# Two stages of a seven-product down projection change places in a one-core decoder trunk

## The chip, the cores and the metric

The kernel runs on one NeuronCore of a Trainium2 chip. The metric is the device time of one execution in microseconds (us), the median of the runs shown. A core has engines that work side by side, each on its own list of instructions in its own order: TensorE (PE in the profile) for matmuls, VectorE (DVE), ScalarE (ACT), GpSimd (POOL), and SyncE (SP), which here issues nearly all DMA transfers. Engines wait for each other by semaphores.

## The reference, cut to what matters

The program is a trunk of two layers on 1024 tokens of width 1024. Layer 0 mixes tokens by retention and RWKV-7 heads, layer 1 by sliding-window attention. Each mixer is followed by a dense SwiGLU network, and the end is an RMS norm:

```
def swiglu(h, w_gate, w_up, w_down):
    return (jax.nn.silu(h @ w_gate) * (h @ w_up)) @ w_down
...
        n = rms_norm(h, norm2_g[layer])
        h = h + swiglu(n, ffn_w_gate[layer], ffn_w_up[layer], ffn_w_down[layer])
    return rms_norm(h, final_g)
```

The inner width D_FF is 2816, that is 22 tiles of 128. The change is in the last product, the one with `w_down`, of both layers.

## The kernel before

Activations are kept transposed: 128 features on the partitions, 512 tokens (one half of the sequence) along the free axis. So `h` has eight tiles for each half, `h0` and `h1`, and the hidden activation has 22 for each half, stored in DRAM (`hid`).

**Split operands.** Every fp32 operand of a matmul is split into a high part, which the matmul can take exactly, and the low rest. A product is three matmuls: high by high, high by low, low by high (`prod`, lines 1188 to 1193). The high part of a weight is a cast on ScalarE (line 1378), the low part a subtract on GpSimd (line 1379), both in `vsplit`. The high part of an activation is a cast on ScalarE (line 356), its low part a subtract on GpSimd or on VectorE by turns (line 358), in `split`.

**Seven products for eight.** The down projection takes the weights and the activations as two by two blocks: rows even or odd (output tiles 2i and 2i+1), columns even or odd (hidden tiles 2p and 2p+1), and the two halves of the tokens. A Winograd form needs seven block products instead of eight, with sums of weights and sums of activations. The blocks of a weight are a11, a12, a21, a22; the sums are s1 = a21 + a22, s2 = s1 - a11, s3 = a11 - a21 and s4 = a12 - s2, formed on VectorE (line 1405). The activation sums (`hc`) were formed and split earlier and are read back from DRAM, already split, by `sums8` (line 1384). Plain activations are read raw from `hid` into the tiles `hr` by `plain8` (line 1389) and split then. Activations X stand in a ring of twelve places (`place`; tiles `n` and `ha` in the profile), `hr` has four.

**Groups and stages.** `down` (lines 1408 to 1488) goes through three groups of columns (4, 4 and 3 pairs, `DGROUPS`). Each group has seven stages, and each stage four blocks of output (`dps`), with 4 pairs 12 matmuls of 128x128 by 128x512 for a block and 48 for a stage. The stages before the change:

1. a11 with the plain even tiles of half 0, into PSUM banks A; a copy `u0` of A on ScalarE (line 1442); VectorE forms s1 and s2 of each block.
2. s2 with activation sum 2, into banks B; B + u0 goes to `h1`; VectorE forms s3 = a11 - a21.
3. a12 with the plain odd tiles of half 0, added to banks A; A goes to `h0`; VectorE forms s4 = a12 - s2 in the place of s2.
4. s3 with activation sum 3, added to B.
5. a22 with activation sum 4, added to B.
6. s1 with activation sum 1, into new banks A.
7. s4 with the plain odd tiles of half 1, added to A.

**What sets the order.** The text of `down` gives an order; a scheduler then places the instructions of each engine by a time model of its own, so engines may take work of the next stages ahead of work of this one. DMA issues marked `keep` stay in program order on SP. `behind` puts an instruction behind another: the copies `u0` stand behind the last weight cast of stage 1 (line 1442). Split weights stand in a ring of six tiles (`w` and `wr`). Each DMA holds one of eight semaphores, so that at most eight are under way on SP.

In the first group of a layer the activations of stage 1 and the weights of its first two blocks are prepared ahead, during the last step of the gate and up products (`first_x`). The weights of the down projection (tiles `wd`) are loaded when their memory gets free, near the start of the first group. At that time VectorE still has the last sums of the gate and up products to form (lines 1200, 1250, 1326). Layer 0's first group begins near 1129 us after the start of the span, layer 1's near 2100 us.

Of the kernel before, what the change touches and what calls it, by code (L numbers as in the profile page):

```python
# [13 lines left out]
ALU = mybir.AluOpType  # L14
# [190 lines left out]
class Kern:  # L205
# [462 lines left out]
    def pair(self, u, hf, p):  # L668
# [124 lines left out]
        for w in range(2):  # L793
# [4 lines left out]
            mean = self.t(mp, [P, 32], "vm", 2)[:, :8].rearrange("p (a b) -> p a b", b=2)  # L798
            V.tensor_reduce(out=mean, in_=ps, axis=AX.X, op=ALU.add, negate=True)

# [33 lines left out]
    def unit(self, u, hf, pairs):  # L834
# [10 lines left out]
        for q in range(2):  # L845
            nc.sync.dma_start(DT[64 * q : 64 * q + 64], dn)
        X = self.t(mp, [P, 16, 32], "X", 1)
        Xf = X.rearrange("p a b -> p (a b)")
        G.memset(Xf, 0.0)
# [4 lines left out]
        for j in range(31):  # L854
            n, m = j // 2 + 1, 31 - j
            tv = tmp[:, : n * m].rearrange("p (a b) -> p a b", b=m)
            V.tensor_tensor(
                out=tv, in0=X[:, 0:n, j : j + 1].to_broadcast([P, n, m]),
                in1=DT[:, j : j + 1, j + 1 : 32].to_broadcast([P, n, m]), op=ALU.mult,
            )  # L860
            V.tensor_tensor(out=X[:, 0:n, j + 1 : 32], in0=X[:, 0:n, j + 1 : 32], in1=tv, op=ALU.add)
            if j % 2:
                yield (), 1.9
        for q in range(2):
            nc.sync.dma_start(dg.rearrange("u (i q) t -> q u i t", q=2)[q], X[64 * q : 64 * q + 64])
        if u:
# [541 lines left out]
    def down(self, L, fp, fz, rest, X, first):  # L1408


        op, S = self.vop, self.nc.scalar
        h0, h1 = (self.kt(self.h[hf]) for hf in range(2))
        dps = range(KT // 2)
        j, ends = len(X), []

        def place():
            nonlocal j
            i, j = j % 12, j + 1
            if i >= 8:
                return self.t(fp, [P, 2, HT], "ha", 4, F32R)  # L1420
            return self.t(self.nb, [P, 2, HT], "n8", 8, F32R)

        def plain(hf, f):
            return self.plain8(L, hf, f, place(), self.t(fp, [P, HT], "hr", 4))

        for gi, g in enumerate(DGROUPS):
            n, ps = g[1] - g[0], range(*g)
            ta, tb = ("fffy", "mmrc")[:: 1 - 2 * (gi % 2)]
            s1, u0, a1 = [], [], []
            W = [self.wdown(L, 0, g, fp, "wd0", 5)]  # L1430
            X = X or [plain(0, 2 * p) for p in ps]
            W += [self.wdown(L, 2 * i, g, fp, "wd0", 5) for i in (1, 2, 3)]
            for i in dps:
                W[i] += self.wdown(L, 2 * i + 1, g, fp, "wd1", 5)
            A = [self.pst(t, [P, HT]) for t in ta]
            first += [self.vsplit(W[dp][0]) for dp in dps[len(first) :]]
            cast = self.last_cast
            for dp in dps:
                a11, a12, a21, a22 = W[dp]
                self.prod(A[dp], first[dp], X, True, False)  # L1440
                u0.append(self.t(fz, [P, HT], "u0", 4))
                self.behind(S.copy(u0[dp], A[dp]), cast)
                s1.append(op(self.wsum(fp, n, 4, 8), a21, a22))
                if ends:
                    self.behind(self.last_vop, ends[dp])
                a1.append(a11)
                W[dp][0] = op(self.wsum(fp, n, 4, 8), s1[dp], a11, ALU.subtract)
            X = [self.sums8(L, p, 2, place()) for p in ps]
            B = [self.pst(t, [P, HT]) for t in tb]
            for dp in dps:  # L1450
                self.prod(B[dp], self.vsplit(W[dp][0]), X, True, False)
                y = op(self.t(fz, [P, HT], "y", 2), B[dp], u0[dp])
                op(h1(2 * dp), h1(2 * dp), y)
                op(W[dp][2], a1[dp], W[dp][2], ALU.subtract)
            X = [plain(0, 2 * p + 1) for p in ps]
            for dp in dps:
                self.prod(A[dp], self.vsplit(W[dp][1]), X, False, True)
                op(h0(2 * dp), h0(2 * dp), A[dp])
                op(W[dp][0], W[dp][1], W[dp][0], ALU.subtract)
            X = [self.sums8(L, p, 3, place()) for p in ps]  # L1460
            for dp in dps:
                self.prod(B[dp], self.vsplit(W[dp][2]), X, False, False)
                y = op(self.t(fz, [P, HT], "y", 2), B[dp], u0[dp])
                op(h1(2 * dp + 1), h1(2 * dp + 1), y)
            X = [self.sums8(L, p, 4, place()) for p in ps]
            while self.owed:
                self.keep(self.nc.sync.dma_start(*self.owed.pop(0)))
            for _ in rest:
                pass
            for dp in dps:  # L1470
                self.prod(B[dp], self.vsplit(W[dp][3]), X, False, True)
                op(u0[dp], B[dp], u0[dp])
                op(h0(2 * dp + 1), h0(2 * dp + 1), u0[dp])
            X = [self.sums8(L, p, 1, place()) for p in ps]
            X6 = [plain(1, 2 * p + 1) for p in ps]
            if g[1] == NP:
                yield
            A = [self.pst(t, [P, HT]) for t in ta]
            for dp in dps:
                self.prod(A[dp], self.vsplit(s1[dp]), X, True, False)  # L1480
                op(h1(2 * dp + 1), h1(2 * dp + 1), A[dp])
            ends, first = [], []
            for dp in dps:
                self.prod(A[dp], self.vsplit(W[dp][0]), X6, False, True)
                op(h1(2 * dp), h1(2 * dp), A[dp])
                ends.append(self.last_vop)
            X = ()
        yield
# [399 lines left out]
```

## Time and profile before

| | |
|---|---|
| median of 3 runs | 2331.51 us (2331.47 to 2333.43) |
| the profiled execution, by its own time | 2330.62 us |
| its span, first to last instruction | 2328.6 us |
| mean granted TensorE clock | 0.996 of full speed |
| DMA, mean over the span | 175 GB/s |

The span lies inside the execution's time, with 2.0 us around it. Times within the trace are counted from the start of the span. In a timeline a row gives start, duration, engine, line, operation, output and inputs, the count, and in brackets the idle time ahead of it with what ended it. Several instructions of a kind in a row stand as one row with a count. A busy TensorE is what the profile models from the starts of the matmuls; where matmuls follow each other without a pause, their starts are a fixed step apart, though each lasts longer than the step.

### The profile page before, as it was taken

The page shows a single profiled execution, that of the slowest core. Times are in us where ns is not written, and L with a number is a line of the kernel's source. Part 1 is how long each engine was busy: PE and PEld are TensorE (multiplying, and loading weights), DVE is VectorE, ACT ScalarE, POOL GpSimd, SP SyncE. Part 2 cuts the span into 40 slices and gives each one's busy share as a digit, 9 for nine tenths or more (in the row PEclk, how much of TensorE's full clock was granted, in tenths as well). Part 3 has the DMA queues.
Part 4 walks back from the last instruction along what each step waited for, and adds up shares of the span by engine and source line. Part 5 has one row for each costly group of instructions (what it writes and reads, how often), then busy time and mean ns, then how long its engine had stood idle before and what let it go on. Part 6 is the DMA issues. An engine that isn't in the chain of part 4 may idle for free.

```text
span 2328.6 us, 35662 instructions
## 1 busy us (share of the span) xinstructions
PE 2289.3 (98%) x13056; PEld 1816.4 (78%) x13056; DVE 1704.2 (73%) x2667; ACT 1044.2 (45%) x1943; POOL 979.8 (42%) x764
## 2 busy tenths in 40 slices
PE   8999999999999999999999999999999999999998
PEld 6777777777778888888788887777788888887886
DVE  6876865875667358888885957877647788888766
ACT  5454434424455333333343456666645333343335
POOL 3132221211341067777776500002102677776775
PEclk9999999999999999999999999999999999999999
DMA  7665553433445555555666331113236466656663
GB/s 276 207 210 194 189 152 127 138 119 112 148 173 191 201 167 207 209 208 214 249 257 216 107 127 64 57 64 122 96 128 224 159 222 218 214 200 252 249 217 113
DMA packets 170622, 407.46 MB, mean 175 GB/s; under 512 B 43216, under 2 KB 45904, under 8 KB 170448
## 3 DMA queue, kind: packets, MB, share of 16 engines
q1 hardware_dynamic: 167040, 398.63, 49.9%
q10 hardware_dynamic: 2832, 4.45, 0.5%
q8 instruction: 104, 1.70, 0.3%
q0 software_dynamic: 576, 2.10, 0.2%
q14 instruction: 70, 0.57, 0.1%
HBM read 276.53 MB, written 123.21 MB: 172 GB/s over the span
## 4 chain that ended last, share of the span: by engine, by line
PE 69%; DVE 5%; ACT 2%; issue 1%; POOL 0%; DMA 0%; DVEq 0%; POOLq 0%; ACTq 0%
PE ps_m L1191 7%; PE ps_m L1192 7%; PE ps_m L1193 7%; PE ps_f L350 4%; PE ps_f L351 4%; PE ps_f L352 4%; PE ps_f L1191 4%; PE ps_f L1193 4%; PE ps_f L1192 4%; PE ps_r L1191 2%; PE ps_r L1193 2%; PE ps_r L1192 2%; PE ps_c L1193 2%; PE ps_c L1192 2%; PE ps_c L1191 2%; PE ps_m L240 2%
## 5 line engine op out<-in xcount | busy, mean ns | idle before, releaser
L240 PE MATMUL ps_f<-n,w 128*128 128x512 f32 x1440 | 379.3, 411 | 8.9 <-ACT w L335 5.7
L240 PEld LDWEIGHTS ps_f<-n,w 128*128 128x128 f32 x1440 | 266.6, 190 | 91.4 <-issue 21.8
L336 POOL TENSOR_TENSOR w<-wr,w 128x512 fp32r<-128x512 f32 x63 | 85.9, 1368 | 523.9 <-ACT w L335 520.1
L335 ACT CAST w<-wr 128x512 fp32r<-128x512 f32 x231 | 142.1, 619 | 178.0 <-PE ps_f L352 76.7
L336 DVE TENSOR_TENSOR w<-wr,w 128x512 fp32r<-128x512 f32 x168 | 120.7, 722 | 68.2 <-ACT w L335 67.9
L336 POOL TENSOR_TENSOR w<-wq,w 128x512 fp32r<-128x512 f32 x91 | 130.3, 1442 | 31.9 <-ACT w L335 31.9
L1191 PE MATMUL ps_m<-n,w 128*128 128x512 f32 x333 | 130.9, 393 | 0.0
L1193 PE MATMUL ps_m<-n,w 128*128 128x512 f32 x333 | 130.2, 391 | 0.4 <-POOL w L1379 0.4
L1192 PE MATMUL ps_m<-n,w 128*128 128x512 f32 x333 | 130.1, 391 | 0.0
L350 PE MATMUL ps_f<-n,w 128*128 128x512 f32 x320 | 127.3, 399 | 0.0
L1200 DVE TENSOR_TENSOR nq<-ps_m,u 128x512 f32<-128x512 f32 x88 | 58.9, 684 | 93.3 <-PE ps_m L1193 93.3
L351 PE MATMUL ps_f<-n,w 128*128 128x512 f32 x320 | 126.9, 396 | 0.0
L352 PE MATMUL ps_f<-n,w 128*128 128x512 f32 x320 | 126.6, 396 | 0.0
L1191 PE MATMUL ps_f<-n,w 128*128 128x512 f32 x287 | 113.7, 396 | 0.0
L1193 PE MATMUL ps_f<-n,w 128*128 128x512 f32 x287 | 112.1, 392 | 0.0
L1192 PE MATMUL ps_f<-n,w 128*128 128x512 f32 x287 | 111.7, 389 | 0.0
L358 POOL TENSOR_TENSOR n<-nq,n 128x512 fp32r<-128x512 f32 x60 | 100.0, 1677 | 7.6 <-ACT n L356 7.6
L1379 POOL TENSOR_TENSOR w<-wd,w 128x512 fp32r<-128x512 f32 (+1 forms) x62 | 85.1, 1379 | 38.9 <-ACT w L1378 37.2
L1191 PE MATMUL ps_m<-cb,w 128*128 128x512 f32 x236 | 91.9, 389 | 0.3 <-DVE nq L1200 0.3
L1379 POOL TENSOR_TENSOR w<-ws,w 128x512 fp32r<-128x512 f32 (+1 forms) x48 | 71.8, 1502 | 47.8 <-ACT w L1378 47.8
L1192 PE MATMUL ps_m<-cb,w 128*128 128x512 f32 x236 | 91.8, 389 | 0.0
L1193 PE MATMUL ps_m<-cb,w 128*128 128x512 f32 x236 | 91.8, 389 | 0.0
(520 smaller groups left out, 6456.9 us busy)
## 6 DMA issues: line engine op xcount, KB each, us to landing
hc<-n SPq DMA_DIRECT2D x84, 512.0 KB, 2.8
wsp<-w SPq DMA_DIRECT2D x54, 512.0 KB, 3.4
w<-wsp SPq DMA_DIRECT2D x54, 512.0 KB, 3.5
n<-hc SPq DMA_DIRECT2D x54, 512.0 KB, 5.6
wq<-in_w_gate SPq DMA_DIRECT2D x44, 512.0 KB, 4.4
u<-u SPq DMA_DIRECT2D x88, 256.0 KB, 3.1
wr<-in_w_in SPq DMA_DIRECT2D x34, 512.0 KB, 4.9
ha<-hc SPq DMA_DIRECT2D x34, 512.0 KB, 5.7
```

The costliest lines, as they stand in the source:

```text
L240: self.nc.tensor.matmul(out, lhsT, rhs, **kw)
L335: nc.scalar.copy(hi[:, :n], raw[:, c])
L336: self.lo.tensor_tensor(out=lo[:, :n], in0=raw[:, c], in1=hi.bitcast(F32)[:, :n], op=ALU.subtract)
L350: nc.tensor.matmul(ps, hi, rh, start=k == 0, stop=False)
L351: nc.tensor.matmul(ps, hi, rl, start=False, stop=False)
L352: nc.tensor.matmul(ps, lo, rh, start=False, stop=k == n - 1)
L358: e.tensor_tensor(out=lo, in0=src, in1=hi.bitcast(F32), op=ALU.subtract)
L1191: mm(ps, hi, xh, start=first and k == 0, stop=False, skip_group_check=True)
L1192: mm(ps, hi, xl, start=False, stop=False, skip_group_check=True)
L1193: mm(ps, lo, xh, start=False, stop=last and k == len(w) - 1, skip_group_check=True)
L1200: self.last_add = V.tensor_tensor(out=o, in0=x, in1=y, op=ALU.add)
L1379: nc.gpsimd.tensor_tensor(out=lo, in0=v, in1=hi.bitcast(F32), op=ALU.subtract)
```

## The change

Stages 2 and 3 exchange their places in all three groups of both layers: the product of a12 with the plain odd tiles of half 0 now follows stage 1, and the product of s2 with activation sum 2 comes third. The sum s3 is now formed in the text with the second stage, s4 with the third.

```diff
                 W[dp][0] = op(self.wsum(fp, n, 4, 8), s1[dp], a11, ALU.subtract)
+            X = [plain(0, 2 * p + 1) for p in ps]
+            for dp in dps:
+                self.prod(A[dp], self.vsplit(W[dp][1]), X, False, True)
+                op(h0(2 * dp), h0(2 * dp), A[dp])
+                op(W[dp][2], a1[dp], W[dp][2], ALU.subtract)
             X = [self.sums8(L, p, 2, place()) for p in ps]
             B = [self.pst(t, [P, HT]) for t in tb]
             for dp in dps:
                 self.prod(B[dp], self.vsplit(W[dp][0]), X, True, False)
                 y = op(self.t(fz, [P, HT], "y", 2), B[dp], u0[dp])
                 op(h1(2 * dp), h1(2 * dp), y)
-                op(W[dp][2], a1[dp], W[dp][2], ALU.subtract)
-            X = [plain(0, 2 * p + 1) for p in ps]
-            for dp in dps:
-                self.prod(A[dp], self.vsplit(W[dp][1]), X, False, True)
-                op(h0(2 * dp), h0(2 * dp), A[dp])
                 op(W[dp][0], W[dp][1], W[dp][0], ALU.subtract)
             X = [self.sums8(L, p, 3, place()) for p in ps]
```

## The prediction

> **What bounds the kernel now.** I read the profile's page first, then windows around the two down projections, then the timelines of the engines there.
>
> ```profile
> span 2328.6 us, 35662 instructions
> PE 2289.3 (98%) x13056; PEld 1816.4 (78%) x13056; DVE 1704.2 (73%) x2667; ACT 1044.2 (45%) x1943; POOL 979.8 (42%) x764
> 1139.70:1144.40 4.70, 2.08 (x8) 0.94 (x6) 4.70 (x6) 1.20 (x2) 2.22 (x3) 1.00 1.04 411
> 1146.00:1340.00 194.00, 194.00 (x857) 160.65 (x856) 153.91 (x179) 77.71 (x137) 133.85 (x93) 1.00 0.56 199
> 2111.00:2115.30 4.30, 1.98 (x9) 1.09 (x7) 4.30 (x6) 1.36 (x3) 1.82 (x3) 1.00 1.04 412
> 2115.30:2118.70 3.40, 3.40 (x9) 2.62 (x10) 3.40 (x3) 0.37 (x1) 3.21 (x2) 0.51 1.03 422
> 2119.00:2300.00 181.00, 181.00 (x800) 149.87 (x799) 141.56 (x158) 75.18 (x130) 127.95 (x90) 1.00 0.57 204
> ```
>
> After the window and its length a row gives PE, PEld, DVE, ACT and POOL busy, then clock, DMA share and GB/s. TensorE is the bound. In the down projections it is fully busy (194.00 of 194.00, 181.00 of 181.00) except right behind the first stage of the first group of each layer. One matmul takes 194.00/857 = 0.226 us. The change touches six groups, but only these two places, with PE busy 2.08 of 4.70 and 1.98 of 4.30, have idle time to win.
>
> ```profile
> 1139.49 0.39 PE L1193 MATMUL ps_y<-n,w 128*128 128x512 f32 x1
> 1139.71 0.39 PE L1191 MATMUL ps_m<-n,w 128*128 128x512 f32 x1
> ...
> 1141.91 0.50 PE L1193 MATMUL ps_m<-n,wr 128*128 128x512 f32 x1 [0.72 <-POOL wr L1379]
> 1144.32 0.50 PE L1191 MATMUL ps_r<-n,wr 128*128 128x512 f32 x1 [1.90 <-ACT wr L1378]
> ```
>
> ```profile
> 2111.09 0.39 PE L1191 MATMUL ps_m<-n,w 128*128 128x512 f32 x1
> ...
> 2112.80 0.50 PE L1193 MATMUL ps_m<-n,w 128*128 128x512 f32 x1 [0.41 <-POOL w L1379]
> 2115.20 0.69 PE L1191 MATMUL ps_r<-n,w 128*128 128x512 f32 x1 [1.90 <-ACT w L1378]
> ```
>
> From the first matmul of stage 2 to the seventh are six steps. Layer 0 took 1144.32 - 1139.71 = 4.61 for 6 x 0.226 = 1.36: **3.25 lost**. Layer 1 took 4.11: **2.75 lost**, and then 3.40 us at clock 0.51, another 3.40 x 0.49 = **1.67**. Together 7.7 us, 0.33%: no gain can be larger.
>
> What ends last there is VectorE, which forms s1, s2 and s3 of each block:
>
> ```profile
> 1133.90:1138.30 4.40, 4.40 (x21) 3.66 (x20) 4.26 (x7) 1.69 (x3) 0.00 (x0) 1.00 1.02 419
> 1131.01 1.67 DVE L1326 TENSOR_TENSOR n<-n,n 128x512 f32<-128x512 f32 x1
> ...
> 1138.33 0.69 DVE L1405 TENSOR_TENSOR ws<-ws,wd 128x512 f32<-128x512 f32 x1
> 1138.94 1.78 DVE L1405 TENSOR_TENSOR wd<-wd,wd 128x512 f32<-128x512 f32 x1
> 1140.65 1.76 DVE L1405 TENSOR_TENSOR ws<-wd 128x512 f32<-128x512 f32 x1
> ...
> 1143.64 0.62 ACT L1378 CAST wr<-ws 128x512 fp32r<-128x512 f32 x1 [3.14 <-DVE ws L1405]
> ```
>
> ```profile
> 1130.38 3.44 POOL L1379 TENSOR_TENSOR w<-wd,w 128x512 fp32r<-128x512 f32 x2
> 1138.38 1.80 POOL L1379 TENSOR_TENSOR w<-ws,w 128x512 fp32r<-128x512 f32 x1 [4.56 <-ACT w L1378]
> 1140.14 1.72 POOL L1379 TENSOR_TENSOR wr<-ws,wr 128x512 fp32r<-128x512 f32 x1
> ```
>
> See two things. While POOL does nothing (0.00 from 1133.90 to 1138.30) VectorE does an operation in 4.26/7 = 0.61 us; beside a POOL subtract the same kind takes 1.78 and 1.76. And a subtract beside VectorE takes 1.72 (3.44/2). So where both work without pause, each finishes about one operation in 1.72. POOL's pause of 4.56 us is what lets VectorE reach s2 of the second block by 1139.02.
>
> **The change part by part.** No operation is added or removed: 48 matmuls, 4 weight casts and subtracts, 4 loads change places, and 4 activation splits come a stage earlier. The scheduler decides what that does, so I read the order of the built program. During stage 1 of layer 0 POOL now has six subtracts in a row (four of a12, two of stage 1), then s2 of blocks 0 and 1, then activations X0 and X2 (X1 and X3 are VectorE's). In layer 1 the two of stage 1 come first and the rest in one row. ScalarE has, behind stage 1: copy of u0 of block 3, cast of s2 of block 1, and only then the casts of X0 to X3. That is the new wait: stage 2's own activations stand, on ScalarE and again on POOL, behind a weight sum of the stage that was moved back, and TensorE waits for them.
>
> Stage 2 now adds into the PSUM banks that the copies of u0 read. The last copy runs from 1139.91 (row below), 0.6 long, ahead of X0's cast in any case: no cost.
>
> Loads: the four hr are issued ahead of the four sums, right behind the last weight.
>
> ```profile
> 1139.91 0.59 ACT L1442 COPY u<-ps_y 128x512 f32<-128x512 f32 x1 [0.23 <-PE ps_y L1193]
> 1148.72 1.66 ACT L356 CAST ha<-hr 128x512 fp32r<-128x512 f32 x3
> 1131.36 0.45 SPq L1384 DMA_DIRECT2D n<-hc  x1
> wd<-in_w_down SPq DMA_DIRECT2D x1, 512.0 KB, 5.8
> n<-hc SPq DMA_DIRECT2D x1, 512.0 KB, 6.6
> ```
>
> The last two rows are the last weight's load, issued at 1130.89, and the first sum's, at 1131.36; they land at 1136.7 and 1138.0: 1.3 us per 512 KB, 0.65 for an hr of 256 KB. So X0 lands near 1137.4 and X3 near 1139.3, the first sum 1.3 later; all before their casts. SP's queue keeps its order apart from this exchange. I cost the loads at nothing; the cover is ScalarE's queue, and if that were free X0 could still be cast at 1137.4.
>
> *Layer 0.* POOL: 1130.38 + 6 x 1.72 = 1140.70, no pause. The fourth of them ends at 1137.26; stage 1's last block needs it for its third matmul, nine ahead of the one at 1139.49, at 1137.45. Stage 1 just holds. VectorE has nine operations from 1131.01 to s2 of block 1. At 1.72, 5.6 of them are done by 1140.70; the other three and a bit take 3 x 0.61 and one subtract of POOL in between (1.27, row in (b)): 1143.8 instead of 1139.02. The cast of s2 then starts at 1143.8, that of X0 0.52 later (three casts take 1.66, one 0.62), and 0.62 after that the first matmul can go: 1145.0, **5.3 after stage 1**. Four matmuls (high half of X0 for four blocks) last until 1145.9. X0's low half stands on POOL behind s2 of block 1: 1144.45 + 2 x 1.72 = 1147.9, **2.0 more**. Then 18 matmuls, 4.1, to 1152.0. X1's low half is the ninth VectorE operation after 1143.8: 3.4 of them until POOL pauses at 1144.45 + 3 x 1.72 = 1149.6, the rest at 0.61, 1153.0: **1.0 more**. Sum 8.3 against 3.25: +5.05.
>
> *Layer 1.*
>
> ```profile
> 2105.84 0.59 ACT L1442 COPY u<-ps_f 128x512 f32<-128x512 f32 x1 [2.13 <-PE ps_f L1193]
> 2111.28 0.59 ACT L1442 COPY u<-ps_y 128x512 f32<-128x512 f32 x1 [0.72 <-PE ps_y L1193]
> 2107.28 0.69 DVE L1405 TENSOR_TENSOR ws<-ws,wd 128x512 f32<-128x512 f32 x1
> ```
>
> The four casts of a12 stand behind the copy of 2105.84, so POOL starts at 2107.0 and then has eight subtracts without pause: s2 of block 0 done at 2107.0 + 5 x 1.72 = 2115.6, of block 1 at 2117.3, X0 at 2119.0, X2 at 2120.8. VectorE ends s2 of block 0 at 2107.9 and three operations later, at 1.72, s2 of block 1: 2113.1. X0's cast ends at 2114.25: **3.2** after stage 1's end at 2111.09. Four matmuls, then six of the third stage, the last waiting for 2117.3: **1.0**; then X0's low half: **1.45**; three matmuls; then X1's, the eighth on VectorE: 4.5 at 1.72 until 2120.8, 3.5 at 0.61, 2122.9: **3.15**. Sum 8.8 against 2.75: +6.05.
>
> *Clock.* Layer 1 keeps its 1.67. In layer 0 the trace shows none, with 0.72 and 1.90 idle; with 5.3 it may come. Bounds 0 and +1.67; part of the slow matmuls would stand ahead of another wait, so I take +0.8. The low bound of the term in layer 1 is -1.67, if the gaps fall so that the clock stays.
>
> The page "TensorE: Matmul & The Clock Gate" of the Trainium skill (section "What's actually happening") says the clock halves after an idle window of about 3.4 us and recovers after a busy one. By that rule layer 0 would pay a whole term; layer 1 here fell after idle times of 0.41 and 1.90 alone, and layer 0 did not after 0.72 and 1.90, so the trace does not bear out 3.4 us as the threshold.
>
> *Elsewhere.* In groups two and three plain activations now come in three stages in a row (last, first, second). Six POOL subtracts at 1.72 are 10.3 of a stage of 48 x 0.226 = 10.9: hidden, with 0.5 spare per stage. Cost 0; if the cover fails, some 1 us at each of four places.
>
> **Sum:** 5.05 + 6.05 + 0.8 = +11.9 on the profiled execution's 2330.62 (span 2328.6 and 2.0 around it): 2342.5. The runs' median, 2331.51, is 0.9 higher, so I say **2343**.
>
> **Rivals.**
>
> (a) *The change does what it says*: a block without sums covers VectorE, and VectorE does not suffer from POOL's longer run. It decides if VectorE keeps 0.61 beside POOL. Then only the fixed order holds. Layer 0: copy at 1139.91, two casts, 0.5 + 0.5 + 0.62, first matmul 1141.6 (1.85), X0's low half at 1141.05 + 2 x 1.27 = 1143.6 (1.15): 3.0 against 3.25. Layer 1: 2111.28 + 1.64 = 2112.9 (1.85), X0's low half at 2107.0 + 7 x 1.27 = 2115.9 (0.6): 2.45 against 2.75. With the clock unchanged -0.55, with it kept up -2.2: 2329.3 to 2331. For it: loads are in time, a12 needs no sum. Against: 1.78 and 1.76 above. This ends not slower, and it can't reach 0.2% faster.
>
> (b) *VectorE is shut out altogether while POOL runs on*, not one for one.
>
> ```profile
> 1109.90 7.71 DVE L358 TENSOR_TENSOR n<-wq,n 128x512 fp32r<-128x512 f32 x1
> 1109.53 2.54 POOL L358 TENSOR_TENSOR n<-wq,n 128x512 fp32r<-128x512 f32 x2
> ```
>
> This one lasted through a run of POOL operations without pause, which took only 1.27 each (2.54/2). Layer 0 hardly changes (POOL's six end at 1138.0, eight operations follow at 0.61, again about 1143 to 1144). In layer 1 VectorE would wait until 2107.0 + 5 x 1.27 = 2113.4, s2 of block 1 come at 2115.2, X0 at 2116.3, X1 near 2124.4: some 3 more, 2346. Against: in the quoted stage itself the two alternate.
>
> (c) *Clock falls at both places and again after the second gaps*: +1.7 to +3.3 on top, 2344 to 2346.
>
> (d) *The later groups lose their cover* (three plain stages in a row): +4, 2347.
>
> **How the numbers follow.** Forecast 0.66, (a) 0.08, (b) 0.08, (c) 0.12, (d) 0.06. A measurement of this kernel tells about 0.2% (4.7 us) from no change, so "same" ends at 2336.2. A half effect (VectorE at 1.2 instead of 1.72 beside POOL) gives about +6, 2337.5, and is in the forecast's share; with the clock's term at its low bound, 2335. That is the lower end; the upper is (b) and (c) together, 2349. Outside is (a), 0.08, and a little at each end. Of (a) I give 0.01 to faster, should its 2329.3 still come out lower, and 0.07 to same; with 0.02 from the weakest of the forecast: faster 0.01, same 0.09, slower 0.90.
>
> **What would show it.** Right: ahead of the first matmul of line 1191 with ps_f and hr's activations, idle time of 3 to 6 us released by ScalarE (n, line 356); a second wait released by POOL (line 358) and one by VectorE (line 358); sum operations of line 1405 at 1.7 from 1131 to 1140; POOL without pause there. Wrong: X0 cast before the copy at the end of stage 1, VectorE operations at 0.6 to 0.7 beside POOL, PE idle under 3.5 us at both places, or new idle time in groups two and three.

## The result, and the profile after

The changed kernel takes **2343.62 us** (median of 6 runs, 2342.48 to 2346.38); the kernel before 2332.79 (6 runs, 2331.47 to 2338.15). The ratio is 1.0048, 95% interval 1.0038 to 1.0059: about 11 us slower (0.0038 to 0.0059 of 2332.79 is 8.9 to 13.8). 2343 was forecast.

First the page of the changed kernel: its span, and the busy times of the engines.

```profile
span 2344.2 us, 35684 instructions
PE 2295.2 (98%) x13056; PEld 1820.7 (78%) x13056; DVE 1696.3 (72%) x2667; ACT 1043.7 (45%) x1943; POOL 984.8 (42%) x764
```

The same 13056 matmuls, the same 2667, 1943 and 764 operations: no work of these kinds was added (the 22 instructions more in all are none of them), so the time is idle time or slow matmuls. One caution on reading the span. The profiled execution itself took 2346.03, 15.4 more than that of before, and 3.9 of this was lost before the down projection was reached, in code that both kernels share. The first activation of layer 0's gate shows it, first in the kernel before, then in the kernel after (timeline of ScalarE; start, duration):

```profile
716.31 0.60 ACT L1246 ACTIVATE sg<-ps_f 128x512 f32<-128x512 f32 x1
```

```profile
720.24 0.60 ACT L1246 ACTIVATE sg<-ps_f 128x512 f32<-128x512 f32 x1
```

So times below are compared within a stage, never from the start of the span.

The windows of the kernel after: length, then PE, PEld, DVE, ACT and POOL busy, clock, DMA share, GB/s.

```profile
1143.60:1149.20 5.60, 0.29 (x2) 0.00 (x0) 5.57 (x6) 2.20 (x5) 2.93 (x3) 1.00 1.03 421
1149.29:1152.70 3.41, 2.69 (x6) 1.68 (x7) 3.41 (x3) 1.51 (x3) 3.41 (x3) 0.50 1.02 419
1152.70:1156.10 3.40, 3.40 (x10) 2.64 (x9) 3.40 (x5) 0.00 (x0) 1.02 (x1) 0.51 0.24 99
1160.00:1350.00 190.00, 190.00 (x840) 157.34 (x839) 142.22 (x173) 74.24 (x130) 127.52 (x88) 1.00 0.55 195
2120.40:2124.80 4.40, 0.15 (x1) 0.00 (x0) 4.37 (x3) 1.70 (x4) 4.40 (x4) 1.00 1.02 417
2124.88:2128.90 4.02, 4.02 (x11) 3.15 (x12) 3.99 (x4) 1.51 (x3) 4.02 (x3) 0.58 0.86 351
...
2132.50:2135.90 3.40, 3.37 (x8) 2.67 (x9) 1.78 (x3) 0.00 (x0) 0.00 (x0) 0.53 0.00 0
2136.00:2310.00 174.00, 174.00 (x769) 144.07 (x768) 123.49 (x147) 67.07 (x116) 120.73 (x83) 1.00 0.59 212
```

TensorE does nothing for 5.60 us in layer 0 and 4.40 in layer 1, where VectorE is busy throughout (5.57 of 5.60, 4.37 of 4.40). Behind that come stretches with a clock of 0.50 to 0.58, two of them in each layer. From 1160 and from 2136 TensorE is fully busy again, through groups two and three: the later groups cost nothing. The timeline of TensorE in the kernel after names what ended its waits:

```profile
1149.29 0.80 PE L1191 MATMUL ps_f<-n,w 128*128 128x512 f32 x1 [5.41 <-ACT n L356]
...
1152.09 0.79 PE L1192 MATMUL ps_f<-n,w 128*128 128x512 f32 x1 [0.72 <-POOL n L358]
...
2120.16 0.39 PE L1193 MATMUL ps_y<-n,w 128*128 128x512 f32 x1
2124.88 1.20 PE L1191 MATMUL ps_f<-n,w 128*128 128x512 f32 x3 [4.33 <-ACT n L356]
...
2132.53 0.79 PE L1192 MATMUL ps_f<-n,w 128*128 128x512 f32 x1 [2.81 <-DVE n L358]
```

Before, the waits at these places were 0.72 and 1.90, and 0.41 and 1.90. The chain behind the first wait of layer 0, from the timelines of ScalarE, then VectorE, then GpSimd in the kernel after:

```profile
1145.76 0.58 ACT L1442 COPY u<-ps_y 128x512 f32<-128x512 f32 x1
1148.10 0.62 ACT L1378 CAST w<-ws 128x512 fp32r<-128x512 f32 x1 [1.77 <-DVE ws L1405]
1148.63 2.17 ACT L356 CAST n<-hr 128x512 fp32r<-128x512 f32 x4
```

```profile
1141.68 1.78 DVE L1405 TENSOR_TENSOR ws<-wd 128x512 f32<-128x512 f32 x1
1143.49 1.65 DVE L1405 TENSOR_TENSOR ws<-ws,wd 128x512 f32<-128x512 f32 x1
1145.07 0.68 DVE L1405 TENSOR_TENSOR wd<-wd,wd 128x512 f32<-128x512 f32 x1
...
1146.38 1.63 DVE L1405 TENSOR_TENSOR ws<-ws,wd 128x512 f32<-128x512 f32 x1
```

```profile
1139.46 5.13 POOL L1379 TENSOR_TENSOR w<-wd,w 128x512 fp32r<-128x512 f32 x3
1145.93 1.54 POOL L1379 TENSOR_TENSOR w<-ws,w 128x512 fp32r<-128x512 f32 x1 [1.33 <-ACT w L1378]
```

Read from the bottom. GpSimd runs without pause until 1144.6 (1139.46 + 5.13). VectorE's operations take 1.65 to 1.78 until then, 0.68 in GpSimd's pause behind it, and 1.63 again beside GpSimd's next subtract (1145.93). The last row of VectorE, s2 of the second block, is done at 1148.01; its cast starts at 1148.10, having waited 1.77 for it; the casts of the activations X, four of them, start at 1148.63 behind that cast; and the matmul at 1149.29 waited for the first of them. A matmul that needs no sum stands still for a sum, because the sum's cast is ahead of its own in ScalarE's queue.

### The profile page after: what moved, and what is told of

It is laid out like the page before. It is cut to its first block, busy times and chain, and to the rows that moved or that the text cites. A ratio compares the mean times of both kernels' runs of the same rounds, so it can differ in the third digit from the quotient of the medians.

```text
span 2344.2 us, 35684 instructions
## 1 busy us (share of the span) xinstructions
PE 2295.2 (98%) x13056; PEld 1820.7 (78%) x13056; DVE 1696.3 (72%) x2667; ACT 1043.7 (45%) x1943; POOL 984.8 (42%) x764
## 4 chain that ended last, share of the span: by engine, by line
PE 79%; DVE 11%; ACT 4%; DMA 3%; issue 2%; SPq 1%; POOL 0%; DVEq 0%; ACTq 0%; POOLq 0%
PE ps_m L1191 8%; PE ps_m L1193 8%; PE ps_m L1192 8%; PE ps_f L240 7%; PE ps_m L240 5%; PE ps_f L350 4%; PE ps_f L351 4%; PE ps_f L352 4%; PE ps_f L1192 4%; PE ps_f L1193 4%; PE ps_f L1191 4%; PE ps_r L1193 2%; PE ps_c L1193 2%; PE ps_r L1192 2%; PE ps_c L1192 2%; PE ps_r L1191 2%
## 5 line engine op out<-in xcount | busy, mean ns | idle before, releaser
L240 PE MATMUL ps_f<-n,w 128*128 128x512 f32 x1440 | 379.4, 412 | 8.8 <-ACT w L335 5.9
L1191 PE MATMUL ps_f<-n,w 128*128 128x512 f32 x309 | 123.4, 401 | 9.7 <-ACT n L356 9.7
L350 PE MATMUL ps_f<-n,w 128*128 128x512 f32 x320 | 127.0, 399 | 0.0
L351 PE MATMUL ps_f<-n,w 128*128 128x512 f32 x320 | 127.0, 397 | 0.0
L352 PE MATMUL ps_f<-n,w 128*128 128x512 f32 x320 | 126.6, 396 | 0.0
L1192 PE MATMUL ps_f<-n,w 128*128 128x512 f32 x309 | 121.4, 393 | 3.5 <-DVE n L358 2.8
L1191 PE MATMUL ps_m<-n,w 128*128 128x512 f32 x318 | 124.6, 392 | 0.0
L1192 PE MATMUL ps_m<-n,w 128*128 128x512 f32 x318 | 123.8, 389 | 0.0
L1193 PE MATMUL ps_m<-n,w 128*128 128x512 f32 x318 | 123.7, 389 | 0.0
L1193 PE MATMUL ps_f<-n,w 128*128 128x512 f32 x309 | 121.2, 394 | 0.0
L1379 POOL TENSOR_TENSOR w<-wd,w 128x512 fp32r<-128x512 f32 (+1 forms) x62 | 90.8, 1472 | 40.0 <-ACT w L1378 39.9
```

Source lines behind the costliest of these rows:

```text
L240: self.nc.tensor.matmul(out, lhsT, rhs, **kw)
L350: nc.tensor.matmul(ps, hi, rh, start=k == 0, stop=False)
L351: nc.tensor.matmul(ps, hi, rl, start=False, stop=False)
L352: nc.tensor.matmul(ps, lo, rh, start=False, stop=k == n - 1)
L1191: mm(ps, hi, xh, start=first and k == 0, stop=False, skip_group_check=True)
L1192: mm(ps, hi, xl, start=False, stop=False, skip_group_check=True)
```

## The experiments

Three questions: at which groups is the time lost; is it the place of X in the queues, or VectorE's slowness, or both; and does an arrangement exist in which the new order pays. **Theory**: only the first group of a layer loses; s2 of block 1 is late because VectorE takes turns with GpSimd's longer run of subtracts, and X stands behind it. **Rivals**: the later groups lose their cover; or the order of the queues alone costs it, however fast VectorE is; or GpSimd's run costs time by itself.

### The exchange in the first group alone

```diff
+            if gi == 0:
+                X = [plain(0, 2 * p + 1) for p in ps]
...
+                X = [self.sums8(L, p, 2, place()) for p in ps]
...
+            else:
+                X = [self.sums8(L, p, 2, place()) for p in ps]
...
+                X = [plain(0, 2 * p + 1) for p in ps]
...
```

> The exchange in the first group of each layer only; groups two and three keep the order of before. Theory (the loss stands right behind the first stage of the first group): as slow as the full change, 10 to 13 us over before, PE idle ahead of X0's matmuls 5.4 us in layer 0 and 4.3 us in layer 1. Rival (the later groups lose their cover by three plain stages in a row): clearly under the full change, 5 us or more of it gone.

Measured: 2343.04 (2338.34 to 2345.36) against 2332.34, ratio 1.0045 [1.0031, 1.0058]. The whole loss. TensorE's timeline in this kernel has the waits of the kernel after, within 0.3 us:

```profile
1147.37 0.79 PE L1191 MATMUL ps_f<-n,w 128*128 128x512 f32 x1 [5.44 <-ACT n L356]
...
2124.09 1.10 PE L1191 MATMUL ps_f<-n,w 128*128 128x512 f32 x3 [4.06 <-ACT n L356]
...
2132.01 0.80 PE L1192 MATMUL ps_f<-n,w 128*128 128x512 f32 x1 [3.08 <-DVE n L358]
```

### The exchange in groups two and three alone

```diff
+            if gi > 0:
+                X = [plain(0, 2 * p + 1) for p in ps]
...
+                X = [self.sums8(L, p, 2, place()) for p in ps]
...
+            else:
+                X = [self.sums8(L, p, 2, place()) for p in ps]
...
+                X = [plain(0, 2 * p + 1) for p in ps]
...
```

> The reverse: the exchange in groups two and three only. Theory: within 2 us of before, PE fully busy in groups two and three. Rival (later groups): 4 us or more over before.

Measured: 2329.86 (2328.82 to 2332.68), ratio 0.999 [0.9981, 0.9999]: no loss, if anything 0.1% gained. The waits of before are back in the first groups (TensorE's timeline of this kernel), and no others are there:

```profile
1143.63 0.50 PE L1191 MATMUL ps_r<-n,wr 128*128 128x512 f32 x1 [1.90 <-ACT wr L1378]
...
2115.36 0.50 PE L1191 MATMUL ps_r<-n,w 128*128 128x512 f32 x1 [1.90 <-ACT w L1378]
```

In this profile the matmul behind the wait in layer 1 lasts 0.50, where before it lasted 0.69 at a clock of 0.51: here the clock did not fall (1.00 from 2115.30 to 2118.70), after the same wait of 1.90. That is one execution, and would be worth the 1.67 of that term; whether it is what the 0.1% consists of stays open.

### The loads of X ahead of the weights

The full change, with the loads `hr` of stage 2 issued ahead of stage 1's loads of wd1 in the first group. The scheduler then expects X earlier and places its casts and subtracts earlier too.

```diff
+            X2 = [plain(0, 2 * p + 1) for p in ps] if gi == 0 else None
             for i in dps:
                 W[i] += self.wdown(L, 2*i+1, g, fp, "wd1", 5)
...
-            X = [plain(0, 2 * p + 1) for p in ps]
+            X = X2 or [plain(0, 2 * p + 1) for p in ps]
```

> The full change, and in the first group the four raw activations of stage 2 are loaded ahead of the second half of the weights (a21, a22). They land about 2.6 us after the first half instead of last, so the scheduler can place their splits ahead of s2. Theory (the time is lost because the splits of X0 to X3 stand behind s2's on ScalarE, POOL and VectorE): the idle time behind stage 1 falls from 5.6 and 4.5 us to 0 to 2.5 in each layer, and the whole is between 4 us under and 1 us over before. Rival (POOL's and VectorE's amount of work in that stretch sets the time, wherever the splits stand): still 6 us or more over before.

Measured: 2329.16 (2325.35 to 2332.84), ratio 0.9989 [0.998, 0.9998], 14.5 less than the changed kernel. ScalarE's timeline of this kernel, TensorE's, and VectorE's:

```profile
1138.12 2.18 ACT L356 CAST n<-hr 128x512 fp32r<-128x512 f32 x4
...
1142.03 0.59 ACT L1443 COPY u<-ps_y 128x512 f32<-128x512 f32 x1 [1.25 <-PE ps_y L1193]
```

```profile
1144.49 0.50 PE L1192 MATMUL ps_f<-n,w 128*128 128x512 f32 x1 [1.32 <-POOL n L358]
...
2113.75 0.49 PE L1191 MATMUL ps_y<-n,wr 128*128 128x512 f32 x1 [1.99 <-ACT u L1443]
2115.08 0.50 PE L1192 MATMUL ps_f<-n,w 128*128 128x512 f32 x1 [0.84 <-POOL n L358]
```

```profile
1144.90 1.77 DVE L1405 TENSOR_TENSOR ws<-ws,wd 128x512 f32<-128x512 f32 x1
```

The four casts of X now lie ahead of the last copy of u0, not behind s2, and the wait of 5.41 is gone. What is left are waits of 1 to 2 us: for X0's low half, and in layer 1 for the copy of u0, which stands behind a weight cast of s2 on ScalarE: the same head of a queue in another place. VectorE is as slow here as in the kernel after: in layer 0 its operations take 1.59 to 1.78 from 1133.1 to 1146.6, the row of 1144.90 among them. Once X no longer stands behind the sums, no wait of layer 0 comes from that; in layer 1 the cast ahead of the copy of u0 had waited 1.69 for s2. GpSimd's long run by itself costs no more than the waits of 1.32 and 0.84.

### GpSimd's pause filled, in the kernel before

Four subtracts whose results nobody uses, in the first group's stage 1, are meant to fill the pause of 4.56 us that GpSimd had in the kernel before. The order of the stages is that of before.

```diff
+            for dp in dps if gi == 0 else ():
+                v = self.t(fz, [P, HT], "y", 2).rearrange("p (k c) -> p k c", c=P)
+                self.nc.gpsimd.tensor_tensor(out=v, in0=W[dp][0], in1=W[dp][1], op=ALU.subtract)
```

> The order of before, with four more POOL subtracts of 128x512 in the first group of each layer, in its pause during stage 1; their results are not used, the computation is unchanged. Theory (VectorE's sums slow from 0.6 to 1.7 us each beside POOL): the sums of line 1405 take about 1.7 us there, s2 comes 4 us late or more, and the kernel is 4 to 9 us slower than before although nothing was exchanged. Rival (only the order of the queues counts, POOL's pause does not matter): 0 to 2 us.

Measured: 2340.14 (2338.27 to 2343.64), ratio 1.0039 [1.0026, 1.0053], 7.8 slower by the medians without any stage exchanged. GpSimd's timeline of this kernel, then VectorE's:

```profile
1131.24 5.13 POOL L1440 TENSOR_TENSOR y<-wd 128x512 f32<-128x512 f32 x3
```

```profile
1138.51 1.76 DVE L1405 TENSOR_TENSOR ws<-wd 128x512 f32<-128x512 f32 x1
```

The filling operations take 1.71 each beside VectorE, and VectorE's sum 1.76 beside GpSimd, where in the kernel before seven operations in that pause took 4.26. But not all of the 7.8 is that. TensorE's timeline shows a second way:

```profile
1138.10 0.50 PE L1193 MATMUL ps_f<-n,w 128*128 128x512 f32 x1 [1.90 <-POOL w L1379]
```

Here stage 1's own matmul waits for a weight's low half that stands behind the filling subtracts on GpSimd. The run shows that GpSimd's pause is worth much to the kernel before; it does not split the loss cleanly between the two ways.

### X ahead of s2 in the queues, nothing else moved

The full change, with the casts of s2's weights put behind the last cast of X on ScalarE, and their subtracts behind the last one of X on GpSimd, in the first group. `high`, `low` and `wlow` are the casts and subtracts that `split` and `vsplit` issued last.

```diff
+            high, low = self.high, dict(self.low)
...
-                self.prod(B[dp], self.vsplit(W[dp][0]), X, True, False)
+                w = self.vsplit(W[dp][0])
+                if gi == 0:
+                    self.behind(self.last_cast, high)
+                    self.behind(self.wlow, low[True])
+                self.prod(B[dp], w, X, True, False)
```

> The full change with the same loads, but in the first group the casts and POOL subtracts of s2 are put behind those of X0 to X3. VectorE's order stays: X1 and X3 still stand behind the sums there. Theory (three queues hold the activations back, one behind the other): the wait on ScalarE behind stage 1 falls from 5.6 and 4.5 us to about 1.5, and a wait for VectorE (line 358, X1's low half) of 3 us or more grows in its place, so the whole stays 6 to 12 us over before. Rival (only the two casts on ScalarE cost the time): no more than 2 us over before. Rival (the raw activations land late): the wait behind stage 1 stays 4 us or more, released by the transfer of hr.

Measured: 2345.17 (2343.22 to 2348.2), ratio 1.006 [1.0046, 1.0073], no better than the full change. TensorE's timeline of this kernel, VectorE's, and VectorE's in the kernel after:

```profile
1142.49 0.50 PE L1191 MATMUL ps_f<-n,w 128*128 128x512 f32 x1 [1.19 <-ACT n L356]
...
1153.70 0.80 PE L1192 MATMUL ps_f<-n,w 128*128 128x512 f32 x1 [6.34 <-DVE n L358]
```

```profile
1152.36 0.68 DVE L1405 TENSOR_TENSOR wd<-wd,wd 128x512 f32<-128x512 f32 x1
1152.96 1.29 DVE L358 TENSOR_TENSOR n<-hr,n 128x512 fp32r<-128x512 f32 x2
```

```profile
1156.00 0.68 DVE L358 TENSOR_TENSOR n<-hr,n 128x512 fp32r<-128x512 f32 x1
```

The first wait falls from 5.41 to 1.19: ScalarE's order made most of that wait, as the forecast had it. But it comes back as 6.34 a few matmuls on, for X's low halves on VectorE, which stand behind the sums there. Mended on ScalarE and GpSimd, the wait moves to the queue that was left, VectorE's. Its place there hardly changed: X1's low half starts 12.1 us behind the start of stage 1's last matmul (1140.91) here and 12.5 behind it (1143.50) in the kernel after, and 11.6 in both in layer 1. So the waits ahead of that could be taken away and the time not fall.

### The low halves of a12 on VectorE

The full change, with the four subtracts of a12's weights in the first group taken from GpSimd and given to VectorE, the engine that is late.

```diff
-    def vsplit(self, v):
+    def vsplit(self, v, e=None):
...
-        nc.gpsimd.tensor_tensor(out=lo, in0=v, in1=hi.bitcast(F32), op=ALU.subtract)
+        (e or nc.gpsimd).tensor_tensor(out=lo, in0=v, in1=hi.bitcast(F32), op=ALU.subtract)
...
-                self.prod(A[dp], self.vsplit(W[dp][1]), X, False, True)
+                self.prod(A[dp], self.vsplit(W[dp][1], self.nc.vector if gi == 0 else None), X, False, True)
```

> The full change, but the four low halves of a12 in the first group are formed on VectorE instead of POOL, so POOL has its pause again and VectorE has four operations more. Theory (VectorE's sums suffer from POOL's unbroken run, 1.7 instead of 0.6 us): in spite of four operations more on VectorE the kernel gets faster than the full change by 4 to 8 us, with sums at 0.6 to 0.7 during stage 1. Rival (VectorE's number of operations counts, not its neighbour): 2 to 5 us slower than the full change.

Measured: 2336.57 (2334.73 to 2340.67), ratio 1.002 [1.0011, 1.0029], 7.1 less than the full change. GpSimd's timeline of this kernel, VectorE's, TensorE's, and ScalarE's in layer 1:

```profile
1142.24 2.13 POOL L1379 TENSOR_TENSOR w<-ws,w 128x512 fp32r<-128x512 f32 x1 [4.95 <-ACT w L1378]
```

```profile
1138.36 1.28 DVE L1379 TENSOR_TENSOR wr<-wd,wr 128x512 fp32r<-128x512 f32 x2
1139.57 0.68 DVE L1405 TENSOR_TENSOR ws<-wd 128x512 f32<-128x512 f32 x1
...
1140.77 0.69 DVE L1405 TENSOR_TENSOR ws<-ws,wd 128x512 f32<-128x512 f32 x1
```

```profile
1146.21 0.50 PE L1191 MATMUL ps_f<-n,w 128*128 128x512 f32 x1 [3.65 <-ACT n L356]
```

```profile
2118.96 0.62 ACT L356 CAST n<-hr 128x512 fp32r<-128x512 f32 x1
2119.48 0.62 ACT L1378 CAST w<-ws 128x512 fp32r<-128x512 f32 x1
```

VectorE was given four operations more and its sums came *earlier*: GpSimd has a pause of 4.95 again, VectorE's operations take 0.68 in it, and the first wait falls from 5.41 to 3.65. X1's low half, too, starts 9.6 us (layer 0) and 9.2 us (layer 1) behind the start of stage 1's last matmul, where it was 12.5 and 11.6, with two and three operations more ahead of it on VectorE.

This run holds VectorE's turns with GpSimd responsible, but it separates them from the order of the queues in layer 0 alone. In layer 1 the first wait falls from 4.33 to 1.19; there the scheduler also moved X0's cast ahead of the cast of s2 of block 1 (the last two rows). By the starts of the matmuls the first group loses 1.2 us less in layer 0 and 5.3 less in layer 1. So the run does not split the 7.1 between VectorE's pace and ScalarE's order.

### Both, with one cast of s2 put back

The loads ahead (third experiment), a12's low halves on VectorE (sixth), and the first cast of s2 put behind the last copy of u0, against the wait of 1.99 that the third experiment left.

```diff
-                self.behind(S.copy(u0[dp], A[dp]), cast)
+                self.behind(last := S.copy(u0[dp], A[dp]), cast)
...
-                self.prod(B[dp], self.vsplit(W[dp][0]), X, True, False)
+                w = self.vsplit(W[dp][0])
+                if gi == 0 and dp == 0:
+                    self.behind(self.last_cast, last)
+                self.prod(B[dp], w, X, True, False)
```

> The full change with both cures in the first group: the raw activations loaded ahead of a21 and a22, the low halves of a12 on VectorE; also the first cast of s2 behind the last copy of u0. Theory: no more than 1 us of idle time behind stage 1 in each layer, no fall of the clock there, and 4 to 8 us under before (all that is to be had is 7.8). Rival (VectorE with four more operations becomes the bound in stage 3, where s2 is needed): idle time moves to stage 3, and the whole is no better than with the loads alone (2329).

Measured: **2325.52** (2322.09 to 2328.37), ratio **0.9974** [0.9964, 0.9985], faster than both kernels: 7.4 below before by the medians, 6.1 by the ratio (3.5 to 8.4 by its interval), and 18.1 below the changed kernel. The windows of this kernel over the down projections, first groups included:

```profile
1130.00:1350.00 220.00, 219.98 (x969) 181.48 (x968) 177.05 (x217) 92.07 (x162) 138.30 (x95) 1.00 0.60 212
2100.00:2290.00 190.00, 190.00 (x839) 157.04 (x838) 147.73 (x175) 76.02 (x134) 130.78 (x91) 1.00 0.62 224
```

TensorE has no idle time there and a full clock. Most of the 7.7 that the prediction called the most that could be gained is gained, with the exchanged stages; what the exchange lacked were X in time and GpSimd's pause. No run mends the order of before in a like way, so it stays open whether the gain needs the exchange at all.

## Why the prediction was right, point by point

The direction, the size and the place were right. Time beyond one step of 0.2266 us per matmul, added up over the starts of TensorE's matmuls around the first groups of the kernel after, stands beside the forecast so:

| us | forecast | measured |
|---|---|---|
| layer 0, waits | 5.3 + 2.0 + 1.0 = 8.3 | 5.56 + 1.12 = 6.68 |
| layer 0, slow clock | 0.8 | 2.73 |
| layer 1, waits | 3.2 + 1.0 + 1.45 + 3.15 = 8.8 | 4.49 + 2.98 = 7.47 |
| layer 1, slow clock | 1.67 | 3.28 |
| sum | 19.6 | 20.2 |

The same count of the kernel before gives 7.8 (its forecast terms: 3.25 + 2.75 + 1.67), so the cost is 12.3 by the traces, 11.9 by the forecast, and 10.8 [8.9, 13.8] by the runs. The sum is right partly because two errors of about 3 us cancel: the waits came out 2.9 smaller (14.2 for 17.1), the slow matmuls 3.5 dearer (6.0 for 2.5). In part that is one effect, since slow matmuls ahead of a wait for a fixed time shorten it; that the two sizes nearly match is luck.

- *First wait of layer 0*, 5.3: held, 5.56, by the chain that was forecast, row by row. The fifth experiment shows ScalarE's order in it, the sixth VectorE's turns with GpSimd (3.65 with the order unchanged).
- *First wait of layer 1*, 3.2: mis-sized, 4.49. The forecast let s2 of block 0 end by 2107.9 at the fast rate, though GpSimd's run of eight was to start at 2107.0, ahead of that sum's own start at 2107.28. VectorE's timeline of the kernel after has four slow operations, not three, up to s2 of block 1:

```profile
2116.59 1.67 DVE L1405 TENSOR_TENSOR ws<-ws,wd 128x512 f32<-128x512 f32 x1
2118.19 1.78 DVE L1405 TENSOR_TENSOR wd<-wd,wd 128x512 f32<-128x512 f32 x1
2119.89 1.76 DVE L1405 TENSOR_TENSOR ws<-wd 128x512 f32<-128x512 f32 x1
2121.68 1.64 DVE L1405 TENSOR_TENSOR ws<-ws,wd 128x512 f32<-128x512 f32 x1
```

- *The second waits*, for GpSimd, 2.0 in layer 0 and 1.0 and 1.45 in layer 1: too large, 1.12 and none. The order of who is late was right, but matmuls at half the clock reach the place later: the time is paid as slow matmuls in place of a wait. In layer 1 the first wait, 1.3 longer than forecast, had paid for part of it too.
- *The waits for VectorE's low halves*: 1.0 in layer 0 did not show, for the same reason; 3.15 in layer 1 was 2.98.
- *Clock*: the term that failed most. Rival (c), with 0.12, is what happened in the records: slow at both places, and again behind the second gap of layer 1. It didn't add to the total as (c) said, because most of the slow matmuls stood ahead of other waits (the last stretch of layer 1, 1.6, did not); the forecast had named that offset for layer 0 alone.
- *Rivals (a) and (b)*: did not happen. VectorE's sums took 1.6 to 1.8 beside GpSimd's run, neither 0.61 nor a standstill.
- *Later groups, loads, PSUM banks at no cost*: held. The first experiment has the whole loss and the second none, and TensorE is busy for 190.00 of 190.00. The copy of u0, nil in the change itself, did cost 1.99 in the third experiment, once nothing else was later.
- *No gain can be larger than 7.7*: not contradicted; the last experiment took 7.4 of it by the medians, 6.1 by the ratio.

## What to carry to other kernels

A block that "needs nothing" still needs its operands prepared, and on engines that take their work in order it waits for whatever stands ahead of that preparation: follow the moved work through every queue before moving the matmuls. Where two engines slow each other, the pause of one is a resource of the other; giving a late VectorE four operations more, so that GpSimd had its pause back, made it earlier. And mending one queue moved the wait to the next (1.19, then 6.34): the loads ahead took the loss away, and only loads, queue and pause mended together left no idle time.

## What the runs showed of the hardware

**Taking turns.** On 128x512 fp32 operands in SBUF, VectorE and GpSimd working at once finish an operation each in about 1.7 us in the stages shown, where they take 0.61 and 1.27 apart. Together they do 2 operations in 1.7; one after the other these would take 1.9, so working side by side gains little over taking turns. The page "SBUF — State Buffer" of the Trainium skill (section "SBUF: two separate sides") says that VectorE and GpSimd share a pair of ports under a lock held for a whole instruction. The durations agree with that roughly, 1.7 being a little less than 1.9; no run here shows the lock itself.

They do not always go one for one. The 7.71 us operation of VectorE in the kernel before is one exception, and the sixth experiment has the reverse in layer 1: a subtract of GpSimd lasted 4.67 while VectorE did six operations of 0.68 or 0.69.

```profile
2116.94 4.67 POOL L1379 TENSOR_TENSOR wr<-ws,wr 128x512 fp32r<-128x512 f32 x1 [5.83 <-ACT wr L1378]
```

And an operation of VectorE with an operand in PSUM (line 1200, at 1130.07 in the kernel after) took 0.69 beside a GpSimd subtract of 1.31 (1129.99).

**The clock.** The forecast counted one fall, in layer 1, and gave 0.8 to one in layer 0. It fell in both and twice in layer 1: to 0.50 and 0.51 for two stretches of 3.4 us behind the wait of 5.41, to 0.58 behind 4.33 (a stretch of 4.02, with some faster matmuls at its end), and again to 0.53 behind 2.81, after only some matmuls at the full rate. It had fallen behind 0.41 and 1.90 in layer 1 of the kernel before, and did not behind 0.43 and 1.90 at the same place in the second experiment:

```profile
2112.95 0.51 PE L1193 MATMUL ps_m<-n,w 128*128 128x512 f32 x1 [0.43 <-POOL w L1379]
```

So the same waits can have it either way. In the sixth experiment the wait of 3.65 was followed by four matmuls at the full rate, and slow ones came only behind the next wait, of 1.60. That the window against which idleness is judged runs freely, as the Trainium skill's page "TensorE: Matmul & The Clock Gate" (section "What's actually happening") says, would explain that; no run here shows the window itself.
